# First two chunks of the input projection share four pairs of row blocks, first x loads on ScalarE's queue, three dummy matmuls ahead: a hybrid encoder layer on one core

## The chip, the cores and the metric

One core of a Trainium2 chip runs the whole layer in float32. The time is the device time of one execution in microseconds (us), the median of three runs. TensorE (PE) multiplies, VectorE (DVE) and ScalarE (ACT) work on tiles in on-chip memory, GpSimd (POOL) only fills constants, and SyncE (SP) issues nearly all DMAs. Each engine takes its instructions strictly in the order of the program.

## What is computed

One encoder layer on 256 tokens of width 2048. Cut to what matters:

```python
hn = rms_norm(h, g_mix_pre)                  # (256, 2048)
u = hn @ w_in                                # w_in: 2048 x 5120 = [q | k | v | x | gate]
attn = neighborhood_attention(q, k, v, rpb)
rec = rglru_bidirectional(xr, ...) * gelu(yg)
mixed = concat(rms_norm(attn), rms_norm(rec)) @ w_out
h = h + rms_norm(mixed)
fn = rms_norm(h)
ff = (silu(fn @ w_ffn_gate) * (fn @ w_ffn_up)) @ w_ffn_down
h = h + rms_norm(ff)
gate = sigmoid(rms_norm(h) @ w_ple_gate)
h = h + rms_norm(gate * (p @ w_ple_proj))
```

## The kernel before, in words

**Products.** A product of two float32 matrices is made of three products of rounded halves: each operand is split into `hi` (the value rounded to the format in which TensorE is fast) and `lo` (the rest), and hi·hi, hi·lo and lo·hi are summed in PSUM (lines 550 to 552; 559 to 561 in the groups of the feed-forward part). Weights come from HBM as tiles `wr` of two row blocks by 512 columns (512 KB, line 477). ACT rounds a tile to `wh` (line 502), DVE subtracts to get `wl` (line 512), and PE uses both. Four buffers hold raw tiles, six hold `wh` and `wl`.

**Chunks.** The input projection goes by ten chunks of 512 columns, each over all 16 row blocks in eight pairs, so eight tiles a chunk. A chunk's two PSUM banks (one for each 128 tokens) are called `acc`; one tile takes 12 matmuls of 128x512 (2 row blocks, 2 halves of the tokens, 3 products). Chunk 0 makes the recurrent input x, chunk 1 makes v, then come q, k and the rest. The first tile is loaded and split in two halves of 256 KB.

**The activations.** x is loaded twice. Transposed and by pairs of row blocks it is `xs` (line 659): `make_hT` multiplies it with the gain and splits it into `hT_hi` (ACT, line 305) and `hT_lo` (DVE, line 307), 128x256 for a row block. As rows it is `xn` (line 667): `norm_x` squares and sums it (ACT, line 697) to get `rstd_x`, which every chunk needs when it is read out of PSUM (line 807 for chunk 0). In the kernel before, the load of pair k of `xs` stands just ahead of weight tile k on SP's queue for k = 0 to 7, and the four loads of `xn` stand ahead of tiles 8 to 11.

**What sets the order.** The program is written by a planner (`Plan`) that keeps a clock for each engine by cost formulas. PE's main work is a fixed list (`seg` for chunks, `Group` for the feed-forward part). All other work is in tasks (generators); whenever PE's planned clock has moved on, the planner emits the tasks' steps that can start before it, the one with the smallest start plus `late` first. So `late` (`LATE`, `TURN_LATE`, `LATE_EVAC`, `URGENT`, `SOON`) is a priority: the more negative, the earlier the step is put on its engine's list. `TURN_LATE` is the priority of a block transpose's trip through DRAM (`turn`, lines 335 and 343: tile to `via`, `via` back to a tile), `LATE_EVAC` that of reading out the last banks of a feed-forward group.

**Start of the program.** All engines are let go after 0.7 us. SP issues `xs` and weight tiles in turn, ACT issues one small load `vec` (the gains) and then works; DVE and PE wait for what ACT makes. `SP, ACT, DVE` each run their lists in order, so an instruction that waits holds up all that stands behind it on its engine.

Of the kernel before, what the change touches and what calls it, by code (L numbers as in the profile page):

```python
# [16 lines left out]
P = 128  # L17
# [10 lines left out]
N = 512  # L28
# [32 lines left out]
MM = 0.2267  # L61
LANDED = 2.5
VIA = 2.0
TURN_LATE = -4.0
DOWN = {
    4: ("p2 p6 s0 p8 p10 s4 p12 p14", "p2 p6 s0 p10 s4 p12 p8 p14"),
    3: ("p2 p4 s0 p6 p8 p10", ""),
}
URGENT = -2.0
SOON = -1.5  # L70
SOON_FROM = 4
LATE_SUMS = 0.0
LATE_EVAC = 0.0
EARLY_EVAC = 0.0
FIRST = "ppppspsp"
KINDS = tuple("ppspspsp" if f == "3" else "ppppspsp" for f in "32233233233")
# [162 lines left out]
def layer(ctx: ExitStack, tc: tile.TileContext, a: dict, out: bass.AP):  # L239
    nc = tc.nc  # L240
# [126 lines left out]
    def done(event):  # L367
        event.t = plan.now
# [35 lines left out]
    segs = []  # L404
# [251 lines left out]

    def load_xs(k, j):
        def f():
            nc.sync.dma_start(xs[k][:, j, :], a["xT"][k][:, j, :])
            done(ev_xs[2 * k + j.start])  # L660
            done(ev_xs[2 * k + j.stop - 1])
        return (128 * (j.stop - j.start), f)
# [6 lines left out]
        return (512, f)  # L669

    for k in range(KD // 2):
        for j in pieces(k):
            extra_loads.setdefault((k, j.start), []).append(load_xs(k, j))
    for i in range(2 * NT):
        extra_loads.setdefault((8 + i, 0), []).append(load_xn(i))

    def make_hT(odd):
        for k in range(odd, KD // 2, 2):
# [29 lines left out]
    def decay():  # L708

        lam = cols("lam")  # L710
        la = [const.tile([P, 16], F32, name=f"la{i}") for i in range(4)]
        yield act(16)
        nc.scalar.activation(la[0], lam, AF.Abs)
        yield act(16, EXP)
        nc.scalar.activation(la[0], la[0], AF.Exp, scale=-1.0)
        yield dve(16)
        nc.vector.tensor_scalar(out=la[1], in0=la[0], scalar1=2.0, scalar2=None, op0=ALU.add)
        yield dve(16)
        nc.vector.reciprocal(la[1], la[1])
        yield dve(16)  # L720
        nc.vector.tensor_tensor(out=la[1], in0=la[0], in1=la[1], op=ALU.mult)
        yield dve(16)
        nc.vector.tensor_tensor(out=la[2], in0=la[1], in1=la[1], op=ALU.mult)
        yield dve(16)
        nc.vector.memset(la[3], 1.0 / 17.0)
        for m in (15, 13, 11, 9, 7, 5, 3, 1):
            yield dve(16)
            nc.vector.tensor_tensor(out=la[3], in0=la[3], in1=la[2], op=ALU.mult)
            yield dve(16)
            nc.vector.tensor_scalar(  # L730
                out=la[3], in0=la[3], scalar1=1.0 / m, scalar2=None, op0=ALU.add
            )
        yield dve(16)
        nc.vector.tensor_tensor(out=la[3], in0=la[3], in1=la[1], op=ALU.mult)
        yield dve(16)
        nc.vector.tensor_scalar(
            out=la[0], in0=lam, scalar1=-1.0, scalar2=0.0, op0=ALU.mult, op1=ALU.max
        )
        yield dve(16)
        nc.vector.scalar_tensor_tensor(  # L740
            out=c8, in0=la[3], scalar=2.0, in1=la[0], op0=ALU.mult, op1=ALU.add
        )
        yield dve(16)
        nc.vector.tensor_scalar(out=nc8, in0=c8, scalar1=-C_RG, scalar2=None, op0=ALU.mult)
        yield dve(16)
        nc.vector.tensor_scalar(out=c8, in0=c8, scalar1=C_RG, scalar2=None, op0=ALU.mult)
        done(ev_c8)

    t1 = {}
    p1_ctx = ExitStack()  # L750
# [439 lines left out]
    def start_biases():  # L1190
        plan.add(load_biases(), plan.clk["pe"])

    for n, (n0, post) in enumerate((
        (O_X, xr_post(0)), (O_V, v_post(0)), (O_Q, qk_post(0, "q")), (O_K, qk_post(0, "k")),
        (O_X + N, xr_post(1)), (O_Q + N, qk_post(1, "q")),
        (O_K + N, qk_post(1, "k")), (O_V + N, v_post(1)), (O_G, yg_post(0)), (O_G + N, yg_post(1)),
    )):
        late = SOON if n >= SOON_FROM else 0.0
        seg(Chunk(post, (open_p1, second_tiles)[n] if n < 2 else None, late), "w_in", n0, hT, KS,
            after=start_biases if n == 3 else None)  # L1200


    t2 = {}
# [599 lines left out]
    for n in range(4):  # L1803
        big_w[i0 + n] = (big_part(n, 0), big_part(n, 1), ev_big)

    plan.add(load_stream())
    plan.add(hi_stream(), late=lambda: lateness(at_hi))
    plan.add(lo_stream(), late=lambda: lateness(at_lo))
    plan.add(sum_stream(), late=lambda: lateness(at_sum))
    plan.add(make_hT(0), late=-2 * LATE)  # L1810
    plan.add(make_hT(1), late=-2 * LATE)
    plan.add(norm_x())
    plan.add(decay())
    with tc.manual_schedule():
        flip = False
        for n, s in enumerate(segs[:-1]):
            if isinstance(s, Group):
                run_group(s, flip)
                flip = not flip
                continue  # L1820
            run_seg(s)
            if n == 9:
                ev_in.t = plan.clk["pe"]
            if n == len(segs) - 5:
                ev_big.t = plan.clk["pe"]
        chunk, lhs, ks, _, _, _, i0 = segs[-1]
        open_chunk(chunk)
        for t in range(NT):
            order = list(range(8)) if t == 0 else [4, 5, 6, 7, 0, 1, 2, 3]
            for n, m in enumerate(order):  # L1830
                products(i0 + m, ks[m][1], lhs, chunk.accs, [t], n == 0, n == 7, chunk.at)
            plan.add(finish(t, chunk), plan.clk["pe"] + plan.SEM)
            plan.run()
        for e in ends:
            plan.reach(e)
# [66 lines left out]
```

## Time and profile before

| | |
|---|---|
| median of 3 runs | 1162.35 us (1161.85 to 1163.66) |
| the profiled execution's own time | 1161.84 us |
| its span, first to last instruction | 1160.0 us |
| time outside the span | 1.84 us |
| TensorE busy | 1139.0 us, 98% of the span |
| VectorE, ScalarE busy | 950.4 us, 697.5 us |

Times in the views count from the first instruction. A row of the timeline has the start, the duration, the engine, the line of the kernel, the operation, out<-in, the shape, the count, and in brackets the idle time of the engine ahead of it with what ended it. A matmul's duration contains the way through the array, so matmuls overlap: the pace is the distance of their starts. "SPq" and "ACTq" are the queues' DMA issues.

### The profile page before, as it was taken

The page shows a single profiled execution, that of the slowest core. Times are in us where ns is not written, and L with a number is a line of the kernel's source. Part 1 is how long each engine was busy: PE and PEld are TensorE (multiplying, and loading weights), DVE is VectorE, ACT ScalarE, POOL GpSimd, SP SyncE. Part 2 cuts the span into 40 slices and gives each one's busy share as a digit, 9 for nine tenths or more (in the row PEclk, how much of TensorE's full clock was granted, in tenths as well). Part 3 has the DMA queues.
Part 4 walks back from the last instruction along what each step waited for, and adds up shares of the span by engine and source line. Part 5 has one row for each costly group of instructions (what it writes and reads, how often), then busy time and mean ns, then how long its engine had stood idle before and what let it go on. Part 6 is the DMA issues. An engine that isn't in the chain of part 4 may idle for free.

```text
span 1160.0 us, 14499 instructions
## 1 busy us (share of the span) xinstructions
PE 1139.0 (98%) x5133; PEld 942.0 (81%) x5133; DVE 950.4 (82%) x1216; ACT 697.5 (60%) x929; POOL 1.6 (0%) x13
## 2 busy tenths in 40 slices
PE   7999999999999999999999999999999999999996
PEld 5888888887887888888888888888888888888885
DVE  6678678879658899999877889998987999987763
ACT  6767868775648645565454555556444556566752
POOL 0000000000000000000000000000000000000000
PEclk9999999999999999999999999999999999999998
DMA  8877767465974868687675675668675667883841
GB/s 299 310 223 219 245 187 244 150 203 148 339 265 135 317 209 270 193 266 240 204 226 172 221 231 182 209 226 266 206 236 181 210 204 238 316 275 128 273 145 72
DMA packets 83304, 257.67 MB, mean 222 GB/s; under 512 B 8992, under 2 KB 24480, under 8 KB 81824
## 3 DMA queue, kind: packets, MB, share of 16 engines
q1 hardware_dynamic: 83088, 256.67, 68.3%
q8 instruction: 40, 0.66, 0.2%
q14 instruction: 32, 0.26, 0.1%
q10 hardware_dynamic: 144, 0.08, 0.0%
HBM read 242.04 MB, written 14.68 MB: 221 GB/s over the span
## 4 chain that ended last, share of the span: by engine, by line
PE 86%; DMA 5%; DVE 4%; ACT 3%; issue 1%; SPq 1%; DVEq 0%; ACTq 0%
PE c L551 14%; PE c L552 14%; PE c L550 14%; PE acc L551 9%; PE acc L552 9%; PE acc L550 9%; PE p L561 3%; PE p L560 3%; PE p L559 3%; PE c L561 2%; PE c L560 2%; PE c L559 2%; DVE wl L512 2%; DMA ev<-via 1%; DMA wr<-in_w_in 1%
## 5 line engine op out<-in xcount | busy, mean ns | idle before, releaser
L512 DVE TENSOR_TENSOR wl<-wr,wh 128x1024 fp32r<-128x1024 f32 (+1 forms) x319 | 368.8, 1171 | 76.9 <-ACT wh L502 75.7
L502 ACT CAST wh<-wr 128x1024 fp32r<-128x1024 f32 (+1 forms) x319 | 317.5, 1011 | 168.8 <-PE c L552 62.7
L550 PE MATMUL c<-wh,hT_mix_hi 128*128 128x512 f32 x436 | 170.1, 390 | 0.0
L551 PE MATMUL c<-wl,hT_mix_hi 128*128 128x512 f32 x436 | 169.8, 389 | 0.0
L552 PE MATMUL c<-wh,hT_mix_lo 128*128 128x512 f32 x436 | 169.7, 389 | 0.0
L550 PE MATMUL acc<-wh,hT_hi 128*128 128x512 f32 x320 | 127.2, 397 | 7.2 <-ACT wh L502 7.2
L502 ACT CAST wh<-lent_t 128x1024 fp32r<-128x1024 f32 x65 | 68.0, 1053 | 106.6 <-DVE lent_t L536 65.8
L551 PE MATMUL acc<-wl,hT_hi 128*128 128x512 f32 x320 | 126.6, 396 | 0.9 <-DVE wl L512 0.9
L552 PE MATMUL acc<-wh,hT_lo 128*128 128x512 f32 x320 | 125.9, 394 | 0.0
L551 PEld LDWEIGHTS c<-wl,hT_mix_hi 128*128 128x128 f32 x436 | 81.8, 188 | 17.2 <-DVE wl L512 0.4
L552 PEld LDWEIGHTS c<-wh,hT_mix_lo 128*128 128x128 f32 x436 | 81.8, 188 | 17.2 <-DVE hT_mix_lo L307 0.2
L550 PEld LDWEIGHTS c<-wh,hT_mix_hi 128*128 128x128 f32 x436 | 81.9, 188 | 16.8
L512 DVE TENSOR_TENSOR wl<-lent_t,wh 128x1024 fp32r<-128x1024 f32 x65 | 78.1, 1220 | 11.0 <-ACT wh L502 10.5
L502 ACT CAST wh<-lent_r 128x1024 fp32r<-128x1024 f32 (+1 forms) x61 | 59.0, 980 | 34.5 <-PE c L552 25.3
L550 PEld LDWEIGHTS acc<-wh,hT_hi 128*128 128x128 f32 x320 | 60.9, 190 | 19.4 <-ACT wh L502 7.2
L512 DVE TENSOR_TENSOR wl<-lent_r,wh 128x1024 fp32r<-128x1024 f32 (+1 forms) x61 | 68.4, 1130 | 8.2 <-ACT wh L502 8.1
L551 PEld LDWEIGHTS acc<-wl,hT_hi 128*128 128x128 f32 x320 | 60.8, 190 | 15.3 <-DVE wl L512 3.2
L552 PEld LDWEIGHTS acc<-wh,hT_lo 128*128 128x128 f32 x320 | 60.9, 190 | 12.6
L550 PE MATMUL acc<-wh,hT_ffn_hi 128*128 128x512 f32 x112 | 44.1, 393 | 0.0
L552 PE MATMUL acc<-wh,hT_ffn_lo 128*128 128x512 f32 x112 | 43.7, 390 | 0.0
L551 PE MATMUL acc<-wl,hT_ffn_hi 128*128 128x512 f32 x112 | 43.6, 389 | 0.0
L550 PE MATMUL c<-wh,mid1h 128*128 128x512 f32 x88 | 34.2, 389 | 0.0
(442 smaller groups left out, 2216.0 us busy)
## 6 DMA issues: line engine op xcount, KB each, us to landing
wr<-in_w_in SPq DMA_DIRECT2D x79, 512.0 KB, 4.8
wr<-in_w_ffn_down SPq DMA_DIRECT2D x70, 512.0 KB, 4.6
wr<-in_w_ffn_gate SPq DMA_DIRECT2D x64, 512.0 KB, 4.6
wr<-in_w_ffn_up SPq DMA_DIRECT2D x64, 512.0 KB, 4.2
wr<-in_w_out SPq DMA_DIRECT2D x32, 512.0 KB, 4.9
wr<-in_w_ple_gate SPq DMA_DIRECT2D x32, 512.0 KB, 4.4
lent_r<-in_w_ffn_up SPq DMA_DIRECT2D x24, 512.0 KB, 4.3
lent_r<-in_w_ffn_gate SPq DMA_DIRECT2D x24, 512.0 KB, 4.5
```

The costliest lines, as they stand in the source:

```text
L502: nc.scalar.copy(his[i][:, j, :], raws[i][:, j, :])
L512: nc.vector.tensor_tensor(out=los[i][:, j, :], in0=raws[i][:, j, :], in1=f32(his[i][:, j, :]), op=ALU.subtract,)
L550: nc.tensor.matmul(accs[t], hi[t], wh[:, j, :], start=st, stop=False)
L551: nc.tensor.matmul(accs[t], hi[t], wl[:, j, :], start=False, stop=False)
L552: nc.tensor.matmul(accs[t], lo[t], wh[:, j, :], start=False, stop=sp)
L559: nc.tensor.matmul(o, lh, wh, start=start, stop=False)
L560: nc.tensor.matmul(o, lh, wl, start=False, stop=False)
L561: nc.tensor.matmul(o, ll, wh, start=False, stop=stop)
```

## The change

- **Turns.** For row-block pairs 0 to 3 the matmuls of chunk 0 and chunk 1 alternate tile by tile; then chunk 0 does its pairs 4 to 7, then chunk 1. Both chunks' banks are open from the start. The loads of `xs` move with it: pairs 0 to 3 stand ahead of tiles 0, 2, 4, 6, pairs 4 to 7 ahead of tiles 8 to 11.
- **ACT's queue.** The loads of `xs` for pairs 0 and 1 (three DMAs) are issued by ACT instead of SP.
- **Dummies.** DVE zeroes 128x512 of a not yet used buffer (`xn[0]`), and three plain float32 matmuls of 128x512 on it go ahead of all others on PE. Nobody reads their result.
- **Norm.** `norm_x` gets a priority of -1.5; the loads of `xn` stand ahead of tiles 11 to 14 instead of 8 to 11.
- **Priorities.** `TURN_LATE` from -4 to -6, `LATE_EVAC` from 0 to -0.5.

```diff
-TURN_LATE = -4.0
+TURN_LATE = -6.0
+TURNS = 4
+XN_FROM = 11
+WARM = 3
+NORM_X = -1.5
-LATE_EVAC = 0.0
+LATE_EVAC = -0.5
...
     def load_xs(k, j):
         def f():
-            nc.sync.dma_start(xs[k][:, j, :], a["xT"][k][:, j, :])
+            (nc.scalar if k < 2 else nc.sync).dma_start(xs[k][:, j, :], a["xT"][k][:, j, :])
...
     for k in range(KD // 2):
-        for j in pieces(k):
-            extra_loads.setdefault((k, j.start), []).append(load_xs(k, j))
+        i = 2 * k if k < TURNS else k + TURNS
+        for j in pieces(i):
+            extra_loads.setdefault((i, j.start), []).append(load_xs(k, j))
     for i in range(2 * NT):
-        extra_loads.setdefault((8 + i, 0), []).append(load_xn(i))
+        extra_loads.setdefault((XN_FROM + i, 0), []).append(load_xn(i))
...
+    def warm_up():
+        some = xn[0][:, 0:N]
+        nc.vector.memset(some, 0.0)
+        to = bank("warm").rearrange("p a s -> p (a s)")
+        for _ in range(WARM):
+            nc.tensor.matmul(to, some[:, 0:P], some, start=True, stop=True)
...
-        seg(Chunk(post, (open_p1, second_tiles)[n] if n < 2 else None, late), "w_in", n0, hT, KS,
-            after=start_biases if n == 3 else None)
+        chunk = Chunk(post, (open_p1, second_tiles)[n] if n < 2 else None, late)
+        if n < 2:
+            firsts.append((chunk, n0))
+        if n == 1:
+            for k in KS[:TURNS]:
+                for ch, c0 in firsts:
+                    seg(ch, "w_in", c0, hT, [k], first=k == KS[0], last=False)
+            for ch, c0 in firsts:
+                seg(ch, "w_in", c0, hT, KS[TURNS:], first=False)
+        elif n:
+            seg(chunk, "w_in", n0, hT, KS, after=start_biases if n == 3 else None)
...
+    warm_up()
...
-    plan.add(norm_x())
+    plan.add(norm_x(), late=NORM_X)
```

Apart from the three dummies and the turns, PE's list is the same. On DVE, ACT and SP the order differs in the first tenth of the lists and in small places of the feed-forward part, where near neighbours change place; between the two (from the second pair of chunks to the feed-forward part's beginning) the lists are the same.

ScalarE's list at the start of the program, before (`L502` makes `wh`, `L305` makes `hT_hi`):

```order
L281 DMA vec<-in_vecs 128x152
L713 ACT_TABLE_LOAD
L713 ACTIVATE la_96<-vec 128x16
L305 ACTIVATE hT_hi<-xs_80,vec 128x256 x2
L502 CAST wh<-wr 128x512
L305 ACTIVATE hT_hi<-xs_80,vec 128x256 x2
L502 CAST wh<-wr 128x512
L305 ACTIVATE hT_hi<-xs_80,vec 128x256 x2
L502 CAST wh<-wr 128x1024
```

The same place in the changed kernel, whose lines are numbered 4 higher there (`L506` makes `wh`, `L309` makes `hT_hi`, `L663` loads `xs`):

```order
L285 DMA vec<-in_vecs 128x152
L663 DMA xs_80<-in_xT 128x256
L718 ACT_TABLE_LOAD
L718 ACTIVATE la_101<-vec 128x16
L309 ACTIVATE hT_hi<-xs_80,vec 128x256
L663 DMA xs_80<-in_xT 128x256
L309 ACTIVATE hT_hi<-xs_80,vec 128x256
L506 CAST wh<-wr 128x512
L663 DMA xs_80<-in_xT 128x512
L506 CAST wh<-wr 128x512
L506 CAST wh<-wr 128x1024
L309 ACTIVATE hT_hi<-xs_80,vec 128x256 x2
```

The load of the second row block now stands behind the first `hT_hi`, and the load of the second pair behind the first `CAST`; the first full tile is cast before the third and fourth `hT_hi`.

VectorE's list at the start, before (`L307` makes `hT_lo`, `L512` makes `wl`):

```order
L307 SCALAR_TENSOR_TENSOR hT_lo<-xs_80,vec,hT_hi 128x256 x2
L512 TENSOR_TENSOR wl<-wr,wh 128x512
L307 SCALAR_TENSOR_TENSOR hT_lo<-xs_80,vec,hT_hi 128x256 x4
L512 TENSOR_TENSOR wl<-wr,wh 128x512
L307 SCALAR_TENSOR_TENSOR hT_lo<-xs_80,vec,hT_hi 128x256 x2
L512 TENSOR_TENSOR wl<-wr,wh 128x1024
```

The same place in the changed kernel:

```order
L756 MEMSET xn_82 128x512
L311 SCALAR_TENSOR_TENSOR hT_lo<-xs_80,vec,hT_hi 128x256 x2
L516 TENSOR_TENSOR wl<-wr,wh 128x512 x2
L311 SCALAR_TENSOR_TENSOR hT_lo<-xs_80,vec,hT_hi 128x256
L516 TENSOR_TENSOR wl<-wr,wh 128x1024
L311 SCALAR_TENSOR_TENSOR hT_lo<-xs_80,vec,hT_hi 128x256
L516 TENSOR_TENSOR wl<-wr,wh 128x1024
```

Both halves of tile 0 now come before the third `hT_lo`, but `wl` of tile 1 stands behind that third `hT_lo`, which belongs to the second pair of row blocks.

ScalarE's list at the end of `norm_x`, before (`L697` squares, `L363` is the root, `L807` reads chunk 0 out of PSUM):

```order
L697 ACTIVATE xn_83,ss_x<-xn_83 128x1024
L502 CAST wh<-wr 128x1024 x6
L363 ACT_TABLE_LOAD
L363 ACTIVATE rt_x<-tot_x,eps 128x2
L807 ACTIVATE ev<-acc_102,rstd_x 128x4x128
L807 ACTIVATE ev<-acc_103,rstd_x 128x4x128
```

The same place in the changed kernel:

```order
L702 ACTIVATE xn_83,ss_x<-xn_83 128x1024
L367 ACT_TABLE_LOAD
L367 ACTIVATE rt_x<-tot_x,eps 128x2
L819 ACTIVATE ev<-acc_107,rstd_x 128x4x128
L819 ACTIVATE ev<-acc_108,rstd_x 128x4x128
L506 CAST wh<-wr 128x1024 x4
```

The six casts that stood between the last square and the root now stand ahead of the last square or behind the two reads of PSUM.

More of the change, by code (lines that the diff above doesn't have):

```diff
@@ L1191, in start_biases @@
         plan.add(load_biases(), plan.clk["pe"])
+    firsts = []
     for n, (n0, post) in enumerate((
@@ L1198, in layer @@
         late = SOON if n >= SOON_FROM else 0.0
-        seg(Chunk(post, (open_p1, second_tiles)[n] if n < 2 else None, late), "w_in", n0, hT, KS,
-            after=start_biases if n == 3 else None)
+        chunk = Chunk(post, (open_p1, second_tiles)[n] if n < 2 else None, late)
[9 more added lines that the diff above has]
+            seg(chunk, "w_in", n0, hT, KS, after=start_biases if n == 3 else None)
+    last_in = len(segs) - 1
     t2 = {}
@@ L1821, in layer @@
             run_seg(s)
-            if n == 9:
+            if n == last_in:
                 ev_in.t = plan.clk["pe"]
```

## The prediction

> **What bounds the kernel now.** I read the page first, then busy time by stage, PE's waits, and the first 20 us row by row on PE, ACT, DVE and SP.
>
> ```profile
> span 1160.0 us, 14499 instructions
> PE 1139.0 (98%) x5133; PEld 942.0 (81%) x5133; DVE 950.4 (82%) x1216; ACT 697.5 (60%) x929; POOL 1.6 (0%) x13
> ```
>
> Busy time by stage (stretch, its length, PE's busy time, then the other engines, the granted clock, DMA share and GB/s):
>
> ```profile
> 7.23:15.81 8.58, 8.03 (x17) 5.54 (x18) 6.99 (x12) 6.94 (x12) 0.00 (x0) 1.00 0.97 344
> 15.81:60.00 44.19, 44.19 (x196) 36.60 (x195) 30.87 (x56) 32.00 (x41) 0.00 (x0) 1.00 0.92 310
> 60.00:300.00 240.00, 237.05 (x1149) 197.57 (x1149) 189.90 (x264) 177.39 (x276) 0.00 (x0) 1.00 0.67 206
> 300.00:1150.00 850.00, 849.59 (x3775) 702.31 (x3773) 717.19 (x875) 475.14 (x590) 0.00 (x0) 1.00 0.68 222
> 1150.00:1160.00 10.00, 0.16 (x1) 0.00 (x0) 4.44 (x8) 3.08 (x6) 0.00 (x0) 0.62 0.27 105
> ```
>
> PE is the bound. From 15.81 to 60 it never stops, from 60 to 300 it idles 240.00 - 237.05 = 2.95 us, from 300 to 1150 only 0.41. The last 10 us are the read-out of the last chunk, which the change leaves alone. So time can only come from the start: 7.23 us without a matmul, and 8.58 us for the first 17. PE's waits (what waited, on what, us in total, times, longest):
>
> ```profile
> PE acc L550 <- ACT wh L502: 7.2, 1, 7.2
> PE acc L551 <- DVE wl L512: 1.5, 4, 0.6
> PE pg L358 <- DVE gl L301: 0.7, 1, 0.7
> ```
>
> And PE's first matmuls:
>
> ```profile
> 7.23 0.80 PE L550 MATMUL acc<-wh,hT_hi 128*128 128x512 f32 x1 [7.23 <-ACT wh L502]
> 7.96 0.80 PE L551 MATMUL acc<-wl,hT_hi 128*128 128x512 f32 x1
> ...
> 10.26 0.63 PE L550 MATMUL acc<-wh,hT_hi 128*128 128x512 f32 x1
> 11.44 0.79 PE L551 MATMUL acc<-wl,hT_hi 128*128 128x512 f32 x1 [0.55 <-DVE wl L512]
> ...
> 14.16 0.63 PE L551 MATMUL acc<-wl,hT_hi 128*128 128x512 f32 x1
> ...
> 15.02 0.63 PE L550 MATMUL acc<-wh,hT_hi 128*128 128x512 f32 x1
> 15.45 0.53 PE L551 MATMUL acc<-wl,hT_hi 128*128 128x512 f32 x1
> 15.81 0.39 PE L552 MATMUL acc<-wh,hT_lo 128*128 128x512 f32 x1
> 16.04 0.39 PE L550 MATMUL acc<-wh,hT_hi 128*128 128x512 f32 x1
> ```
>
> Two paces: 15.45 - 15.02 = 0.43 us from start to start until 15.45, then 16.04 - 15.81 = 0.23 for the rest of the program. The granted clock reads 1.00 in both stretches, so that column doesn't show what makes the first ones slow; only the starts do. Matmul 18 starts at 15.81; at the fast pace it would have stood 17 x 0.227 = 3.86 us behind the first, at 11.09. The 4.72 us between are 0.50 for the first `wl`, 0.95 for the second (10.26 to 11.44 instead of 0.23), and 3.27 for fifteen steps at the slow pace. That, and any change of the first start, is what the change can reach. I follow matmul 14 (14.16), the first that needs `wl` of tile 1, and matmul 18 (15.81), after which nothing waits for a long time.
>
> **The dummies.** Their price is bounded by the one plain float32 product of the program:
>
> ```profile
> 247.40 0.59 PE L953 MATMUL pb_attn<-ssa,ones 128*128 128x256 f32 x2
> 247.64 0.58 PE L550 MATMUL acc<-wh,hT_hi 128*128 128x512 f32 x1
> 248.06 0.40 PE L551 MATMUL acc<-wl,hT_hi 128*128 128x512 f32 x1
> ```
>
> From 247.40 to 248.06 run it and one normal matmul: 0.66 - 0.23 = 0.43 us for 256 columns, 0.86 for 512, and 1.6 at the slow pace (x 0.43 / 0.227). Three take 2.6 to 4.9 us. They wait only for a 128x512 memset, at most the 0.69 us of a DVE pass of that width (row 7.21 below), so they run from about 1.5 (SP's first issue at 0.74 shows when the engines are let go) to 6.4 at the latest. In this trace PE idles until 7.23, so they cost nothing while the first real matmul is later than 6.4. What they bring is the open point: the pace changed 8.2 us after the first matmul, or 4.0 us after PE last stopped (11.44). 4.9 us of dummies are enough by the second reading, not by the first. The page "TensorE: Matmul & The Clock Gate" of the Trainium skill (Part 1) says that full speed comes after one fully busy window of about 3.4 us, whose phase is free-running; by it, 4.9 us hold a whole window in only (4.9 - 3.4) / 3.4, some 4 in 10, of the executions (an estimate from that page; the trace's 4.0 us agrees with a window, the phase no row shows). I take the fast pace for the likelier: the dummies alone last longer than 4.0 us, and the gap of 1.6 us to the first real matmul is followed by more work.
>
> **x on ACT's queue.** This is where the change can hurt itself. ACT, DVE and SP rows of before, then the DMA issues of the first 20 us (KB each, median us from issue to landing):
>
> ```profile
> 3.35 0.22 ACT L713 ACTIVATE la<-vec 128x16 f32<-128x16 f32 x1 [0.90 <-DMA vec<-in_vecs]
> 3.48 0.49 ACT L305 ACTIVATE hT_hi<-xs,vec 128x256 fp32r<-128x256 f32 x1
> 6.16 0.51 ACT L305 ACTIVATE hT_hi<-xs,vec 128x256 fp32r<-128x256 f32 x1 [2.20 <-DMA xs<-in_xT]
> 6.58 0.60 ACT L502 CAST wh<-wr 128x512 fp32r<-128x512 f32 x1
> ```
>
> ```profile
> 7.21 0.69 DVE L512 TENSOR_TENSOR wl<-wr,wh 128x512 fp32r<-128x512 f32 x1
> ...
> 11.74 0.88 DVE L307 SCALAR_TENSOR_TENSOR hT_lo<-xs,vec,hT_hi 128x256 fp32r<-128x256 f32 x2 [0.36 <-ACT hT_hi L305]
> 12.54 1.22 DVE L512 TENSOR_TENSOR wl<-wr,wh 128x1024 fp32r<-128x1024 f32 x1
> ```
>
> ```profile
> 0.74 0.38 SPq L659 DMA_DIRECT2D xs<-in_xT  x1
> ...
> 1.64 0.42 SPq L659 DMA_DIRECT2D xs<-in_xT  x1
> ```
>
> ```profile
> xs<-in_xT SPq DMA_DIRECT2D x7, 256.0 KB, 5.2
> wr<-in_w_in SPq DMA_DIRECT2D x2, 256.0 KB, 3.8
> ...
> xs<-in_xT SPq DMA_DIRECT2D x2, 128.0 KB, 3.5
> vec<-in_vecs ACTq DMA_DIRECT2D x1, 76.0 KB, 2.6
> ```
>
> Before, the second row block's x was issued at 1.64 and used at 6.16. Now it is issued by ACT behind the first `hT_hi`. That one starts at 3.48 or, its x being issued 0.4 us later behind `vec`, up to 0.3 later: 3.7. So the issue is at 3.8. Landing takes between 2.6 (`vec`, alone on ACT's queue) and 3.5 or more (its own size, but behind 256 KB of weights on SP's queue); nearest is `vec`, with more bytes: 3.1, so 6.9. Then by the distances of before: cast of tile 0 at +0.42, first matmul +0.65 later, at 8.0 instead of 7.23; first `wl` and matmul 2 at 6.9 + 1.8 = 8.7. The second pair's x (256 KB) is issued behind that cast, at 7.4. It lands 3.5 us later by the shorter rows, 5.2 by its own row, which is that of a queue with weights ahead; on an empty queue I take 3.6: 11.0. `hT_hi`, one `hT_lo` and `wl` of tile 1 follow: +0.49, +0.44, +1.22, so matmul 14 at 13.2 instead of 14.16; then 4 x 0.227, matmul 18 at 14.1. At the fast pace PE has done its first 13 by then (8.7 + 11 x 0.227 = 11.2) and idles about 2 us: part of what the pace gives is lost to x.
>
> Here the rule that speaks against the edit: by "DMA: Bandwidth & Descriptors" of the Trainium skill (section "Issuing engines are not separate DMA queues"), a second issuing engine saves only issue time, since all share the same DMA engines. In rows that saving is one issue, 0.43 us; the sum by it would leave x to land no sooner after its issue than the 3.5 and 5.2 of before, and matmul 14 at 15.2.
>
> **The turns.** For tiles 0 to 7 a pair of x serves 24 matmuls, 24 x 0.227 = 5.4 us, and 1024 KB of weights and 256 KB of x come in that time: 240 GB/s, below the 344 GB/s of the first stretch; before it was 768 KB in 2.7 us, 290 GB/s. In the 5.4 us ACT casts two tiles and makes two `hT_hi`,
>
> ```profile
> L502 ACT CAST wh<-wr 128x1024 fp32r<-128x1024 f32 (+1 forms) x319 | 317.5, 1011 | 168.8 <-PE c L552 62.7
> ```
>
> so 2 x 1.0 + 2 x 0.5 us, and DVE needs 2 x 1.2 + 0.9. So after matmul 14 I expect no wait: with PE 2 us earlier than before it still isn't ahead of its tiles. Cost nothing.
>
> **Norm and read-out.**
>
> ```profile
> 34.07 1.06 ACT L697 ACTIVATE xn<-xn 128x1024 f32<-128x1024 f32 x1 [0.34 <-DMA xn<-in_x]
> ...
> 44.91 1.28 ACT L363 ACT_TABLE_LOAD   x1
> 46.73 1.27 ACT L807 ACTIVATE ev<-acc,rstd_x 128x512 f32<-128x512 f32 x2 [0.23 <-DVE rstd_x L365]
> ```
>
> Chunk 0 now ends with matmul 144, at 14.1 + 126 x 0.227 = 42.7, and is read at about 43, 3 us sooner than before. The root comes right behind the last square, so even with `xn` 3 us later `rstd_x` is there by 34.1 + 1.1 + 3 + 1.8 (the distance from 44.91 to 46.73), 40.0. New is that ACT waits for chunk 0 with four casts queued behind: tile 14's `wl` comes 0.4 + 1.3 + 1.0 + 1.2 = 3.9 us after matmul 144, and PE needs it 24 matmuls, 5.5 us, after. Hidden, with 1.6 us to spare; if `xn` came that much later than 43, PE would wait. Gain: at most the 0.7 of `pg`, as the recurrent chain starts sooner; I count 0.
>
> **Priorities in the feed-forward part.** PE idles 0.41 us in 850, so there is nothing to gain; a loss needs weights that come late. Moved ahead are trips to DRAM that wait for DVE with weight loads behind them on SP:
>
> ```profile
> SPq L335 <- DVE mid L329: 48.3, 11, 6.2
> ```
>
> Eleven waits, up to 6.2 us, and PE never saw one. Two trips move by one load. From nothing to one such wait (6.2); PE's 0.41 us over all eleven is nearer to nothing: 0.
>
> **Sum.** Matmul 18 comes 15.81 - 14.1 = 1.7 us sooner, the rest of PE's list follows. Own time 1161.84 - 1.7 = 1160.1. The profiled execution is at the lower end of the three runs, 0.5 under the median, and the start of the pace may well be what differs: 1160.6 for the median. A measurement of this kernel tells about 0.2%, 2.3 us, from no change: faster means under 1160.0, slower over 1164.7.
>
> **Rivals.**
>
> 1. *More than that.* x lands 2.6 and 3.2 us after issue (`vec`'s row, and the 3.8 of 256 KB less the time in line): second block at 6.4, second pair issued at 6.9, there at 10.1, matmul 14 at 12.2, and the 0.7 of `pg` goes too. 1.0 + 0.7 more: 1158.9. For it: nothing is ahead on ACT's queue. Against: 0.97 DMA share in that stretch. Chance 0.2.
>
> 2. *The pace isn't cured.* The dummies end at 6.4, PE idles to 8.0, and the slow pace lasts until 8.2 us after the first real matmul, 16.2. Then matmul 14 is at 8.7 + 12 x 0.43 = 13.9, 18 at 15.6 and 20 at 16.4, where before it was at 16.27: 0.1 later. 1161.84 + 0.1 + 0.5 = 1162.4. For it: the 8.2 us of before began with matmul 1 and ran through a stop of 0.55. The page on the clock gate would give this whenever no window was filled. Chance 0.25.
>
> 3. *Slower.* ACT's list serialises x. With 4.5 us (1.64 to 6.16) to the second block and 5.2 to the second pair, the first matmul is at 9.4, the second pair's x is issued at 8.8, lands at 14.0, and matmul 14 is at 16.2, 2.0 later than before. PE has then idled so often that the slow pace lasts 6 us more: 14 steps x 0.2 = 2.8, less 4 x 0.2 that before had there: 1161.84 + 2.0 + 2.0 + 0.5 = 1166.3. At the fast pace it turns to a loss if the second pair's x lands later than 12.7, 5.3 us after issue; only with the slow pace too is it over 0.2%. For it: the medians of 5.2. Against: those stood in line. Chance 0.1.
>
> My forecast, with matmul 14 near 13 and the fast pace, keeps 0.45.
>
> **How the numbers follow.** The forecast spans 1159.3 to 1161.7 (landing 0.7 us either way, 0.5 for the middle); a third of its 0.45 lies under 1160.0. Faster: 0.15 + 0.2 = 0.35. Slower: rival 3, nearly whole, 0.1. Same: 0.55. The range reaches from rival 1 with 0.4 to spare to rival 2 with 1: 1158.5 to 1163.3.
>
> **What would show it.** Right: matmul starts 0.23 apart from the first real one on; the first at about 8.0; a wait of some 2 us for `wl` of tile 1, released by DVE behind `hT_hi` and the second pair's x; no wait from there to 60 us; about 3 us of PE idle between 60 and 300 as before; nothing new after 300. Wrong: 0.43 between starts beyond 13 us; matmul 18 after 15.8; casts that wait for chunk 0 with PE waiting for `wl` at 43 to 50 us; a new wait of PE above 1 us in the feed-forward part.

## The result and the profile after

The changed kernel takes 1163.86 us (median of 21 runs; twenty lie between 1162.88 and 1166.33, one, at a mean granted clock of 0.56 instead of 0.99, at 1938.76), the kernel before 1161.37 (21 runs, 1160.22 to 1164.15) beside it. The ratio is 1.0021, with a 95% interval of 1.0015 to 1.0028: slower by 2.5 us, just over the 2.3 us that the prediction took for the least difference to be told, and outside its range of 1158.5 to 1163.3. The profiled execution took 1163.18 us, 1.34 more than that of before. It lies 0.7 us under its median and that of before 0.5 over its own, so the traces account for 1.34 of the 2.5 us.

The page of the kernel after:

```profile
span 1161.4 us, 14515 instructions
PE 1141.6 (98%) x5139; PEld 943.5 (81%) x5139; DVE 950.2 (82%) x1217; ACT 695.3 (60%) x929; POOL 1.6 (0%) x13
```

TensorE's busy time has grown by 2.6 us and holds 5.2 us of dummies; the span is 1.4 us longer. Busy time by stage (columns as before):

```profile
8.00:15.81 7.81, 4.31 (x10) 3.10 (x11) 4.12 (x7) 5.36 (x9) 0.00 (x0) 0.60 0.51 174
15.81:60.00 44.19, 44.19 (x195) 36.57 (x194) 29.19 (x46) 32.11 (x45) 0.00 (x0) 0.99 0.88 299
60.00:80.00 20.00, 20.00 (x98) 16.86 (x97) 16.97 (x34) 14.42 (x20) 0.00 (x0) 1.00 0.73 252
80.00:300.00 220.00, 217.71 (x1062) 182.17 (x1061) 176.47 (x248) 164.68 (x258) 0.00 (x0) 1.00 0.67 208
```

Until 15.81 us TensorE has started ten matmuls; before, it had started seventeen between 7.23 and there. From 60 to 300 it idles 2.29 us instead of 2.95: the stop for `pg` is gone. So the loss is at the start. TensorE's longest waits, and its first rows:

```profile
PE acc L554 <- ACT wh L506: 4.9, 1, 4.9
PE warm L759 <- DVE xn L756: 1.4, 1, 1.4
PE acc L555 <- DVE wl L516: 1.1, 2, 0.9
PE c L555 <- DVE wl L516: 0.9, 1, 0.9
```

```profile
1.45 5.19 PE L759 MATMUL warm<-xn 128*128 128x512 f32 x6 [1.45 <-DVE xn L756]
11.50 0.79 PE L554 MATMUL acc<-wh,hT_hi 128*128 128x512 f32 x1 [4.86 <-ACT wh L506]
...
15.80 0.63 PE L554 MATMUL acc<-wh,hT_hi 128*128 128x512 f32 x1
16.23 0.50 PE L555 MATMUL acc<-wl,hT_hi 128*128 128x512 f32 x1
16.57 0.40 PE L556 MATMUL acc<-wh,hT_lo 128*128 128x512 f32 x1
...
17.04 0.39 PE L555 MATMUL acc<-wl,hT_hi 128*128 128x512 f32 x1
...
17.96 0.40 PE L556 MATMUL acc<-wh,hT_lo 128*128 128x512 f32 x1
```

The dummies end at 6.64, and TensorE then stands for 4.86 us. The first real matmul is at 11.50 (7.23 before), the steps are 0.43 us until 16.23 and 0.23 from 16.57 on, matmul 14 is at 17.04 without a wait for `wl`, matmul 18 at 17.96 (15.81 before). From matmul 18 to the last one the kernel before takes 1133.96 us (15.81 to 1149.77) and the changed one 1133.19 (17.96 to 1151.15): in these two executions, what is lost is lost ahead of matmul 18. What made it wait stands in ScalarE's rows and in the DMA issues of the first 20 us:

```profile
1.18 0.45 ACTq L663 DMA_DIRECT2D xs<-in_xT  x1
...
4.43 0.22 ACT L718 ACTIVATE la<-vec 128x16 f32<-128x16 f32 x1 [1.49 <-DMA vec<-in_vecs]
5.41 0.51 ACT L309 ACTIVATE hT_hi<-xs,vec 128x256 fp32r<-128x256 f32 x1 [0.76 <-DMA xs<-in_xT]
5.41 0.33 ACTq L663 DMA_DIRECT2D xs<-in_xT  x1
10.43 0.51 ACT L309 ACTIVATE hT_hi<-xs,vec 128x256 fp32r<-128x256 f32 x1 [4.52 <-DMA xs<-in_xT]
10.44 0.33 ACTq L663 DMA_DIRECT2D xs<-in_xT  x1
10.85 2.07 ACT L506 CAST wh<-wr 128x512 fp32r<-128x512 f32 x3
```

```profile
xs<-in_xT ACTq DMA_DIRECT2D x2, 128.0 KB, 4.6
xs<-in_xT ACTq DMA_DIRECT2D x1, 256.0 KB, 2.5
vec<-in_vecs ACTq DMA_DIRECT2D x1, 76.0 KB, 3.7
```

The second row block's x is issued at 5.41, behind the first `hT_hi`, and lands at 10.43: 5.0 us for 128 KB. SP has meanwhile sent five weight loads, 2 MB, without an x between them:

```profile
0.73 2.48 SPq L481 DMA_DIRECT2D wr<-in_w_in  x5
```

The granted clock, 1 us at a time, shows what the wait did to the pace:

```profile
8.00:9.00 1.00, 0.00 (x0) 0.00 (x0) 0.00 (x0) 0.00 (x0) 0.00 (x0) 1.00 0.99 386
9.00:10.00 1.00, 0.00 (x0) 0.00 (x0) 0.00 (x0) 0.00 (x0) 0.00 (x0) 0.82 0.48 175
10.00:11.00 1.00, 0.00 (x0) 0.00 (x0) 0.03 (x1) 0.57 (x2) 0.00 (x0) 0.50 0.02 8
...
16.00:17.00 1.00, 1.00 (x5) 0.81 (x4) 1.00 (x3) 1.00 (x3) 0.00 (x0) 0.77 0.98 164
```

The clock falls to half between 9 and 10 us, inside the wait, and comes back between 16 and 17. The DMA share of 0.02 between 10 and 11 shows that by then all that was issued had come: x was among the last.

### The profile page after: what moved, and what is told of

Same layout as the page of the kernel before. It is cut to its first block, busy times and chain, and to the rows that moved or that the text cites. A ratio compares the mean times of both kernels' runs of the same rounds, so it can differ in the third digit from the quotient of the medians.

```text
span 1161.4 us, 14515 instructions
## 1 busy us (share of the span) xinstructions
PE 1141.6 (98%) x5139; PEld 943.5 (81%) x5139; DVE 950.2 (82%) x1217; ACT 695.3 (60%) x929; POOL 1.6 (0%) x13
## 4 chain that ended last, share of the span: by engine, by line
PE 90%; DVE 4%; ACT 3%; DMA 1%; issue 1%; DVEq 0%; ACTq 0%
PE c L555 13%; PE c L556 13%; PE c L554 13%; PE acc L554 11%; PE acc L556 11%; PE acc L555 11%; PE p L564 3%; PE p L565 3%; PE p L563 3%; PE c L564 2%; PE c L563 2%; PE c L565 2%; DVE wl L516 1%; ACT wh L506 1%; DMA xs<-in_xT 1%
## 5 line engine op out<-in xcount | busy, mean ns | idle before, releaser
L506 ACT CAST wh<-wr 128x1024 fp32r<-128x1024 f32 (+1 forms) x319 | 316.0, 1011 | 148.6 <-PE c L556 46.4
L506 ACT CAST wh<-lent_t 128x1024 fp32r<-128x1024 f32 x65 | 68.1, 1053 | 119.5 <-DVE lent_t L540 86.4
L506 ACT CAST wh<-lent_r 128x1024 fp32r<-128x1024 f32 (+1 forms) x61 | 58.9, 980 | 30.1 <-PE c L556 23.3
L555 PEld LDWEIGHTS acc<-wl,hT_hi 128*128 128x128 f32 x320 | 60.7, 190 | 13.2 <-DVE wl L516 1.1
```

The costliest lines, as they stand in the source:

```text
L506: nc.scalar.copy(his[i][:, j, :], raws[i][:, j, :])
L555: nc.tensor.matmul(accs[t], hi[t], wl[:, j, :], start=False, stop=False)
```

## The experiments

**Theory A**: the loss is x on ACT's queue, and through the wait the lost clock. **Rival B**: the turns and the priorities lose it later in the list. **Rival C**: the dummies change nothing. The table gives, for each kernel, the starts of the first, 14th and 18th real matmul, the time from the 18th to the last matmul (all from the profiled executions, us), and the ratio to the kernel before, measured beside it.

| kernel | 1st | 14th | 18th | 18th to last | ratio, 95% interval |
|---|---|---|---|---|---|
| before | 7.23 | 14.16 | 15.81 | 1133.96 | 1 |
| changed | 11.50 | 17.04 | 17.96 | 1133.19 | 1.0021 (1.0015 to 1.0028) |
| changed, again | 11.52 | 17.53 | 18.45 | 1133.24 | 1.0028 (1.0016 to 1.0040) |
| x back on SP's queue | 6.72 | 10.76 | 11.81 | 1133.64 | 0.9974 (0.9963 to 0.9986) |
| x early on ACT's queue | 8.91 | 14.86 | 15.78 | 1133.60 | 0.9987 (0.9975 to 0.9999) |
| changed, no dummies | 11.56 | 17.19 | 18.11 | 1132.45 | 1.0005 (0.9992 to 1.0018) |
| before + dummies | 6.60 | 13.78 | 15.00 | 1140.14 | 1.0021 (1.0008 to 1.0033) |
| x on SP, no dummies | 6.69 | 12.04 | 12.96 | 1133.40 | 0.9976 (0.9966 to 0.9986) |
| before + x on ACT's queue | 12.61 | 20.21 | 21.92 | 1133.73 | 1.0051 (1.0038 to 1.0063) |
| x on SP, old priorities | 7.40 | 11.44 | 12.47 | 1134.00 | 0.9980 (0.9970 to 0.9989) |
| changed, eight dummies | 11.35 | 15.04 | 16.07 | 1135.49 | 1.0010 (1.0000 to 1.0020) |
| before + turns | 6.30 | 12.31 | 13.37 | 1153.76 | 1.0116 (1.0098 to 1.0134) |
| changed, weights held back | 8.76 | 13.93 | 14.85 | 1135.81 | one run, 1162.76 us |
| before + turns + norm first | 6.83 | 12.36 | 13.29 | 1133.00 | 0.9971 (0.9957 to 0.9984) |
| before + norm first | 6.74 | 14.21 | 15.47 | 1136.07 | 1.0010 (0.9993 to 1.0026) |

The profiled execution is one of the runs. That of "before + dummies" (1167.20 us) lies 2.4 us over its median and that of "before + turns" (1179.16) 3.3; the others lie within 1.4 us of theirs.

**x back on SP's queue**

```diff
-            (nc.scalar if k < 2 else nc.sync).dma_start(xs[k][:, j, :], ...)
+            nc.sync.dma_start(xs[k][:, j, :], ...)
```

> The changed kernel with all x loads back on SP's queue, in line with the weight tiles; turns, dummies, norm and priorities stay. Theory A (x on ACT's queue comes late, because SP issues 2 MB of weights in one go and ACT issues the second and third load only behind its own work): first real matmul at 7 to 7.5 us instead of 11.50, fast pace (0.23 from start to start) from the first one on since PE idles less than 1 us behind the dummies, matmul 14 near 11.5, matmul 18 near 12.5: 5.5 us sooner than in the changed kernel, 3.3 sooner than before; ratio to before 0.997. Rival B (the loss lies in the turns or the priorities, x's queue is only a bystander): no faster than before, ratio 1.001 or more. Rival C (the dummies don't change the pace): first matmul at 7.2 but 0.43 from start to start until about 15 us, ratio 0.999 to 1.000.

Measured 1158.54 us (8 runs) against 1162.22. ScalarE's and TensorE's rows of this kernel:

```profile
5.65 0.51 ACT L309 ACTIVATE hT_hi<-xs,vec 128x256 fp32r<-128x256 f32 x1 [1.71 <-DMA xs<-in_xT]
```

```profile
6.72 0.63 PE L554 MATMUL acc<-wh,hT_hi 128*128 128x512 f32 x1
...
10.76 0.50 PE L555 MATMUL acc<-wl,hT_hi 128*128 128x512 f32 x1 [0.29 <-DVE wl L516]
```

With one word changed the loss of 2.5 us is a gain of about 3: x, issued by SP at 1.64 in line with the weights, is there at 5.65, no stop lies ahead of the first real matmul, and matmul 18 comes 6.15 us sooner. A is borne out, B is not needed for the loss.

**x early on ACT's queue.** The three loads are moved to the head of ACT's list, right behind `vec`; the queue stays ACT's.

```diff
+    for k, j in ((0, slice(0, 1)), (0, slice(1, 2)), (1, slice(0, 2))):
+        nc.scalar.dma_start(xs[k][:, j, :], a["xT"][k][:, j, :])
...
     def load_xs(k, j):
         def f():
-            (nc.scalar if k < 2 else nc.sync).dma_start(xs[k][:, j, :], a["xT"][k][:, j, :])
+            if k >= 2:
+                nc.sync.dma_start(xs[k][:, j, :], a["xT"][k][:, j, :])
```

> As the changed kernel, but ACT issues its three x loads at the head of its list, right behind the gains, instead of behind its first activations and cast. If the place in ACT's list is what makes x late: second block lands by 6, second pair by 8, first matmul at 7 to 7.5, ratio to before 0.997 as with x on SP. If it is the queue itself (weights of SP's queue go ahead of what ACT's queue asks for): the second block still lands at 9 or later, first matmul at 10 or later, ratio 1.001 or more. In between, with fair halves for the two queues: second block at about 6, second pair at 8.

Measured 1161.39 us (11 runs). Its ScalarE and TensorE rows:

```profile
7.84 0.51 ACT L309 ACTIVATE hT_hi<-xs,vec 128x256 fp32r<-128x256 f32 x1 [1.92 <-DMA xs<-in_xT]
```

```profile
8.91 0.80 PE L554 MATMUL acc<-wh,hT_hi 128*128 128x512 f32 x1 [3.11 <-ACT wh L506]
```

So the 4.8 us between 5.65 and 10.43 have two parts. 7.84 - 5.65 = 2.2 us remain with x issued as early as SP issued it: that is the queue beside 2 MB of weights. 10.43 - 7.84 = 2.6 us more come from the place in ScalarE's list. Neither of the two causes that the expectation set against each other is the whole.

**Weights held back.** A small DMA on SP's queue ahead of tile 1, which reads the first `hT_hi` and so waits for it.

```diff
+            if i == 1:
+                yield hT.ev[0]
+                seen = kept.tile([P, 16], F32, name="seen")
+                nc.sync.dma_start(seen, f32(hT_hi[:, 0, 0:16]))
```

> The changed kernel with one more small DMA on SP's queue ahead of the weights of tile 1, which reads the first hT_hi and so holds back the weights of tiles 1 to 3 (1.5 MB) until ScalarE has made it; only the 512 KB of tile 0 are on their way when ScalarE issues the second row block's x. Theory (backlog): the 5.0 us of that load are time behind the weights already issued; now vec and the first x land in 2.6 to 3.2 us, the first hT_hi comes before 4.3 instead of 5.41, the second row block lands within 3.5 us of its issue, and the first real matmul starts at 8 to 9 instead of 11.5. Rival (the queue itself is slow, or the 1.28 us and the order of ScalarE's list decide): 4.5 us or more from issue to landing again and the first matmul after 10. The time of the whole is not what it is for, since the weights come later.

ScalarE's rows of this kernel:

```profile
5.47 0.34 ACTq L667 DMA_DIRECT2D xs<-in_xT  x1
7.69 0.51 ACT L309 ACTIVATE hT_hi<-xs,vec 128x256 fp32r<-128x256 f32 x1 [1.72 <-DMA xs<-in_xT]
```

The same load, issued at the same place and time as in the changed kernel, took 2.2 us instead of 5.0, and the first real matmul came at 8.76: the backlog of weights is what it stood behind. One half of the expectation missed: the first `hT_hi` was still at 5.47, since `vec` again took 3.8 us, though only 512 KB of weights were on their way. (The second pair's x, issued at 7.70 beside the 1.5 MB now released, took 6.0 us: the same loss, one load later.)

**No dummies** (the call of `warm_up` taken out of the changed kernel).

> The changed kernel without the memset and the three dummy matmuls. If the dummies' effect is gone by the time of the first real matmul (11.50, 4.9 us after the last dummy, slow pace until 16.23): same time as the changed kernel, ratio to before 1.002. If the dummies cost something on the way of x or the weights: faster than the changed kernel by up to 0.5 us. If they help at all: slower by 0.5 to 1.5 us.

Measured 1163.46 us (11 runs), first matmul 11.56, steps of 0.43 to 16.72. The rows are those of the changed kernel with 0.1 us added: at the start the dummies were paid back with nothing. By the medians it is 1.2 us slower than before, by the ratio 0.6, and the interval includes no difference. The changed kernel had 1.0021 and, repeated, 1.0028. By the ratios it is thus 1.9 to 2.7 us slower with its dummies than without them, by the medians (1163.86 and 1163.46) only 0.4; the expectation allowed 0.5. So three dummies may cost time that the start doesn't show. The two profiled executions differ by 0.7 us behind matmul 18 (1133.19 against 1132.45).

**Eight dummies.**

```diff
-WARM = 3
+WARM = 8
```

> The changed kernel with eight dummies instead of three, nothing else. Theory: in the changed kernel TensorE reaches full pace at 6.2 us and loses it because it stands from 6.64 to 11.50. Five more dummies at 0.86 us each fill that gap up to about 10.9, before the first real matmul can start (11.5), so they cost nothing and the real matmuls run 0.23 us apart from the first on. Then matmul 14 waits for wl of tile 1, which VectorE has ready at 15.1 (row 13.87 + 1.22), instead of starting at 17.04, and matmul 18 comes at 16.0 instead of 17.96: 2.0 us sooner, ratio 1.0002 to 1.0006 where the changed kernel had 1.0021. Rival: the slow start is not due to the idle time (it comes with the first loads' traffic, or a second drop follows at a later stop); then matmuls are 0.43 us apart after 11.5 again and the ratio stays at 1.002 or more.

Measured 1162.99 us (12 runs) against 1162.15. TensorE's rows:

```profile
1.45 9.48 PE L759 MATMUL warm<-xn 128*128 128x512 f32 x16 [1.45 <-DVE xn L756]
11.35 0.49 PE L554 MATMUL acc<-wh,hT_hi 128*128 128x512 f32 x1 [0.41 <-ACT wh L506]
...
16.07 0.39 PE L556 MATMUL acc<-wh,hT_lo 128*128 128x512 f32 x1
```

With the gap filled the real matmuls run fast from the first on, and matmul 18 is at 16.07, where 16.0 was expected: the slow start after 11.5 is the clock that the wait lost. The ratio moved from 1.0021 to 1.0010, 1.3 us for the 1.9 gained at the start, and not to the 1.0002 to 1.0006 expected; without any dummies it was 1.0005. In the profiled execution nothing is left of the 1.9 us at the last matmul (1151.56), since TensorE idles 3.92 us between 80 and 300 instead of 2.29. The largest stop there is new:

```profile
PE po L360 <- ACT r L901: 1.5, 1, 1.5
```

**Dummies alone**, in the kernel before.

> The kernel before with the memset and the three dummy matmuls alone. If dummies that end 0.6 us before the first real matmul keep the fast pace: matmuls 0.23 apart from 7.2 us on, but weights and x then come just in time (wl of tile 1 to 4 were ready 0.4 to 2 us ahead of use), so 1 to 2.5 us faster than before, ratio 0.998 to 0.999. If the pace isn't changed by them: ratio 1.000, 0.43 between starts until 15 us.

Measured 1164.80 us (12 runs, 1162.14 to 1168.0) against 1162.22: slower, where either outcome expected had it faster or the same. TensorE's rows:

```profile
8.71 0.40 PE L551 MATMUL acc<-wh,hT_hi 128*128 128x512 f32 x1
11.06 0.79 PE L552 MATMUL acc<-wl,hT_hi 128*128 128x512 f32 x1 [1.95 <-DVE wl L513]
11.65 0.63 PE L553 MATMUL acc<-wh,hT_lo 128*128 128x512 f32 x1
```

The pace is fast from matmul 3 on, so C is wrong. But TensorE then runs into the missing `wl` of the next pair sooner, stands 1.95 us, and is slow again until 14.2; matmul 18 gains only 0.8 us. The profiled execution then lost 6 us behind it, with stops ahead of 71.22 (1.25 us, for `gh`) and 72.49 (0.75, for `gl`), behind which the steps were slow again until 75.6. Why these came is open.

**x on SP, no dummies** (the edits of "x back on SP's queue" and "No dummies" together).

> The kernel with x back on SP's queue, turns, norm and priorities kept, without the memset and the three dummies: what the dummies are worth where PE is fed. If they set the fast pace from the start there: without them 0.43 between the starts until 14 to 17 us, some 16 to 20 steps 0.2 us longer, so 3 to 4 us slower than with them, ratio to before 0.999 to 1.001. If turns and x on SP make the gain by themselves: ratio 0.997 as with dummies.

Measured 1158.83 us (9 runs) against 1161.98. No stop, steps of 0.43 only from 6.69 to 11.00, matmul 18 at 12.96. With x in time the dummies still bring 1.15 us at matmul 18 (11.81), which the medians don't tell apart. What gains is something else in the change.

**x on ACT's queue alone**, in the kernel before.

> The kernel before with the first three x loads moved to ACT's queue and nothing else. If ACT's queue alone makes the loss: second block lands at 9 to 10.5, first matmul at 10 to 11.5 instead of 7.2, slow pace until 14 to 17 us, 2.5 to 4 us slower than before, ratio 1.002 to 1.0035. If it needs the turns (more weights ahead): first matmul near 8, ratio 1.000 to 1.001.

Measured 1167.67 us (5 runs), a larger loss than expected. ScalarE's row:

```profile
11.54 0.51 ACT L305 ACTIVATE hT_hi<-xs,vec 128x256 fp32r<-128x256 f32 x1 [5.75 <-DMA xs<-in_xT]
```

Matmul 18 is 6.11 us later than before, and the profiled time 5.8. So this edit by itself costs some 6 us, and the rest of the change gives back more than half of it.

**Old priorities** (x on SP, `TURN_LATE` and `LATE_EVAC` as before).

> The kernel with x back on SP's queue, with the priorities of turn and read-out as before (-4 and 0); turns, dummies and norm stay. If the priorities cost nothing or bring nothing: same as with the new ones, ratio 0.9965 to 0.998, and the wait of about 1 us near 390 us is there in both. If they make that wait: it is gone and the ratio is 0.001 lower.

Measured 1159.91 us (11 runs). The time behind matmul 18 is 1134.00 against 1133.64, and the stop near 386 us is there with and without: `TURN_LATE` and `LATE_EVAC` did nothing that shows.

**The changed kernel again.**

> The changed kernel itself on the chip of these runs, to stand beside them: ratio 1.001 to 1.003, second block of x landing at 10 to 10.5 us, first real matmul at 11 to 11.6.

Measured 1164.37 us (6 runs): the second block issued at 5.46, there at 10.45, first matmul at 11.52. The start repeats.

**Turns alone**: the changed kernel with x on SP, no dummies, and all numbers but `TURNS` as before.

```diff
...
-XN_FROM = 11
+XN_FROM = 8
...
-NORM_X = -1.5
+NORM_X = 0.0
...
```

> The kernel before with nothing but the turns of chunks 0 and 1 (and the loads of xs placed for them): x on SP's queue, no dummies, the loads of xn and all priorities as before. Theory: the turns are what gains in the fed kernels, since they take the stop for the second wl away (0.95 us) and let the slow pace end at 11 instead of 15.5 us; 0.997 to 0.9985 times the kernel before, like the fed kernel without dummies (0.9976). Rival: the norm's priority with the later loads of xn is the gain, for instance by taking the stop of pg (0.65 us) away; then 0.999 to 1.000 and that stop near 67 to 71 us is there in full.

Measured 1175.86 us (4 runs) against 1162.15, and the theory's number fell with it. The start is as expected (matmul 18 at 13.37); the loss comes later. ScalarE's rows, then TensorE's longest waits behind the first:

```profile
50.18 0.29 ACT L367 ACTIVATE rt_x<-tot_x,eps 128x2 f32<-128x2 f32 x1
50.70 1.27 ACT L819 ACTIVATE ev<-acc,rstd_x 128x512 f32<-128x512 f32 x2 [0.23 <-DVE rstd_x L369]
```

```profile
PE acc L555 <- DVE wl L516: 5.2, 2, 3.8
PE acc L554 <- ACT rec_hi L303: 4.3, 1, 4.3
PE pb_rec L965 <- DVE ssr L980: 2.6, 1, 2.6
```

The last square of `xn` is done at 33.4, but the root stands behind nine casts in ScalarE's list and is taken at 50.18. Chunk 0, whose last matmul starts at 41.9 with the turns, is read at 50.70 (46.73 in the kernel before). TensorE idles 15.0 us between 80 and 300, in part for the recurrent chain (`rec_hi`, `ssr`), which starts from that read-out.

This edit changes more than its name says. The planner lays the steps by its clocks, and here it has also laid TensorE's own list anew: from 80 to 290 us other matmuls stand between those of the chunks in some twenty places. Besides this kernel, only "weights held back" and the last one of this section have such a new list; in all others TensorE's order is that of the kernel before, dummies and turns apart. How much of the 15.0 us the late read-out makes and how much the new order is not shown.

**Turns with the norm's priority** (the kernel above with one number more).

```diff
-NORM_X = 0.0
+NORM_X = -1.5
```

> The turns alone (which took 1.0116) with one number more: the norm's priority of -1.5; the loads of xn stay ahead of tiles 8 to 11, the other priorities as before, x on SP's queue, no dummies. Theory: with the turns chunk 0 ends at 40 us, but without the priority its root stood behind nine casts (at 50.2 us) and the read-out of chunk 0, from which the recurrent chain starts, came at 50.7 instead of 42.0; everything that the chain feeds was late and TensorE stood 15 us between 80 and 300. With the priority the root goes ahead of those casts, the read-out comes before 46, the stops of 4.3, 3.8 and 2.6 us vanish, and the ratio is 0.997 to 0.999. Rival: the priorities of the later parts or the place of the loads of xn make those 15 us; then the ratio stays above 1.005.

Measured 1158.81 us (10 runs) against 1162.31. ScalarE's row, and TensorE's where the pace changes:

```profile
41.61 1.37 ACT L819 ACTIVATE ev<-acc,rstd_x 128x512 f32<-128x512 f32 x2 [0.93 <-PE acc L556]
```

```profile
6.83 0.80 PE L554 MATMUL acc<-wh,hT_hi 128*128 128x512 f32 x1 [6.83 <-ACT wh L506]
...
11.13 0.63 PE L554 MATMUL acc<-wh,hT_hi 128*128 128x512 f32 x1
11.56 0.50 PE L555 MATMUL acc<-wl,hT_hi 128*128 128x512 f32 x1
11.90 0.39 PE L556 MATMUL acc<-wh,hT_lo 128*128 128x512 f32 x1
```

Now the read-out waits only for TensorE's last matmuls of the chunk, 9.1 us sooner than with the turns alone, TensorE's list has the order of the kernel before again, and the kernel is 3.5 us faster than before, 2.5 of which are there at matmul 18 (13.29 for 15.81). Turns and priority are all that the gain needs; this is as fast as the best version with dummies (0.9974), and has neither dummies nor x on ACT's queue.

**The norm's priority alone**, in the kernel before.

```diff
-    plan.add(norm_x())
+    plan.add(norm_x(), late=-1.5)
```

> The kernel before with only the norm's priority of -1.5. Theory: in the kernel before chunk 0 ends at 44 us and is read at 46.7, and TensorE stands 2.95 us between 60 and 300, so the priority can bring 2 us there at the most and is worth much only together with the turns: 0.9985 to 1.0005, and the stop for pg (0.65 us) shorter or gone. Rival: the norm's priority is by itself what makes the fed kernels faster; then 0.998 or less.

Measured 1163.84 us (10 runs), no difference that can be told. ScalarE's row:

```profile
38.18 1.26 ACT L807 ACTIVATE ev<-acc,rstd_x 128x512 f32<-128x512 f32 x2 [0.29 <-DVE rstd_x L365]
```

In the kernel before, chunk 0 ends with matmul 96, which starts at 33.5 us and not near 44 as the expectation has it, so the read-out at 46.73 waited only for the norm. Reading it out 8.5 us sooner brings nothing: the stop for `pg` is down to 0.34 us, as expected, but stops of 1.1 (`rec_hi`) and 1.5 us (`wl`, feed-forward part) have come, and here too the planner has laid TensorE's list anew, in some fourteen places between 110 and 280 us. So the priority is worth nothing alone and some 17 us (1175.86 against 1158.81) once the turns are there. An early read-out by itself is not what makes the gain.

## Why the prediction was wrong

- **What bounds the kernel.** Right: the loss and the gains made by feeding TensorE lie ahead of matmul 18. In the changed kernel and in nine of the fourteen other rows of the table the list behind it took 1132.45 to 1134.00 us. It isn't a constant, though: the other five took 1.5 to 20 us longer behind it. Three of them are those whose list for TensorE the planner laid anew (turns alone, norm alone, weights held back); the other two are dummies alone and eight dummies, with the old order.
- **The step that failed: "x on ACT's queue".** It put the issue of the second row block at 3.8 and said "nearest is `vec`, with more bytes: 3.1, so 6.9". Measured: issued at 5.41, landed 5.0 us later, at 10.43. The issue slipped since `vec` took 3.7 us instead of 2.6 and the first x 4.2, so the first `hT_hi` came at 5.41 and not 3.7. The landing slipped because the 3.1 was taken from `vec`, which comes before most weights are sent; by 5.41 SP has sent 2 MB of them. With 1.5 MB of these held back the load took 2.2 us, so the duration belonged to the traffic, not to the queue. So the first matmul came at 11.50 (8.0 predicted) and, at the slow pace, matmul 18 at 17.96 (14.1 predicted): 3.9 us later, where the whole gain forecast was 1.7. Only the second pair's x was quick (2.5 us, 3.6 predicted), since the DMA engines had run dry by then.
- **The dummies.** Their price was near (4.9 us at the most predicted, 5.2 measured), and they did raise the clock: the "gap of 1.6 us" was to be short enough. It was 4.86 us, and the clock fell. The failure follows from the first; with eight dummies or with x in time the pace was as predicted.
- **Rival 3** had the mechanism ("ACT's list serialises x", with the slow pace) and a chance of only 0.1. Its first matmul was 2.1 us too early (9.4 for 11.50), its time 2.4 us too long (1166.3 for 1163.9): it let the slow pace go on behind matmul 14, for 2.0 us net, while in the run the pace was back at 16.57, ahead of matmul 14.
- **The turns** at "Cost nothing", **the norm** at 0: both wrong as single terms, and as a sum, which is a gain of 3.5 us. With the priority a pair of x feeds 24 matmuls, the stop of 0.95 us goes, and steps are slow until about 11 to 11.6 us instead of 15.45. Without the priority the turns lose 13.7 us, with TensorE's list in another order. The prediction's working had it that "The root comes right behind the last square", and set the edit to 0; the root does so only because of the edit. What the edit prevents was never priced. That the time missed the range by only 0.6 us is luck: x on ACT's queue costs some 6 us by itself, and a gain that the sum didn't have gave back more than half of it.
- **Priorities in the feed-forward part** at 0: right. `TURN_LATE` and `LATE_EVAC` changed nothing that shows. The changed kernel has a new stop of 0.91 us at 391 for `wl`, but with the old priorities it is there as well (0.68).
- **The rule that speaks against the edit** ("DMA: Bandwidth & Descriptors" of the Trainium skill, "Issuing engines are not separate DMA queues": a second issuing engine saves only issue time) pointed the right way. The sum by it put matmul 14 at 15.2, nearer to the measured 17.04 than the forecast's 13.2, and still too early: the separate queue wasn't merely without use, the weights went ahead of x.

What stays open: why eight dummies and dummies alone, and perhaps three in the changed kernel, lose time behind the start, in the first two between 60 and 300 us. But for the dummies and their memset the order of every engine's instructions is that of the changed kernel and of the kernel before, so it isn't another order that loses it. The new stops are mostly for steps of the recurrent and attention chains (`po`, `sc`, `pg`); that TensorE is now ahead of ScalarE and VectorE there is only argued. Nor is it settled why `vec` lands 1.1 us later as soon as x leaves SP's queue.

## What to carry to other kernels

In these runs the landing time of a load was that of the traffic it met, 2.2 us without and 5.0 to 6.2 with 2 MB of weights issued by another queue: before moving a small urgent load to another queue, count what the first queue will send in its absence, and what the new issuing engine must do before it gets to the load. Where two edits are made for each other (turns that feed TensorE sooner but end chunk 0 later, 41.9 for 33.5, and a priority that has the norm ready by then), a trial of each alone misleads: one gave nothing here and the other 1.2% more time, both together 0.3% less. Where a planner writes the lists, look first whether a trial of one edit still has the order of the others: these two had not. A clock raised by dummies was lost here where no real work was there when they ended, and where it was, they brought 1.15 us at matmul 18 and nothing that the medians show.

## What the runs showed that was not expected

- **The clock falls after short stops.** The stop ahead of the real work was 1.26 us in the kernel with old priorities, and the steps stayed at 0.23; with 1.95 us (dummies alone), 2.12 (weights held back), 3.11 (x early on ACT's queue) and 4.86 us (changed) they went to 0.43. Later in the lists two stops close together did it as well: 1.25 and 0.75 us (dummies alone, at 71 and 72 us), 1.18 and 0.63 (turns alone, 277 and 279), 1.10 and 0.75 (norm alone, 282 and 284); one stop of 1.50 us (eight dummies, 221) did not. "TensorE: Matmul & The Clock Gate" of the Trainium skill (Part 1) has the slow state after an idle window of about 3.4 us; 1.95 us in one piece, or 1.81 in two, was enough here.
- **The granted clock shows a fall but not the first slow stretch.** It reads 1.00 up to 9 us in the changed kernel, dummies at a slow pace among them (three took 5.19 us, where the five that eight have more took 4.29), and 0.50 from 10 to 16; in the kernel before it reads 1.00 beside steps of 0.43.
- **Two queues did not share evenly.** At the 386 GB/s between 8 and 9 us an even half would move 128 KB in 0.7 us, which beside the 2.2 us without a backlog would make under 3; with 2 MB on SP's queue such a load took 5.0 us (changed) and 6.2 (issued early, 1.65 to 7.84). The packets' times show where it was lost: of the load issued at 5.41 nothing moves until 8.5 us, while SP's queue moves some 200 KB in each half microsecond; its 128 KB go between 8.5 and 10. In the kernel with x early both queues move side by side, ACT's with 29% of the bytes from 5 to 8 us. What decides between the two the traces don't show.
